# Feed-forward products combined in PSUM, operand order by first use, and gated tiles split early, in a two-layer FP32 trunk on one core

## The chip, the cores and the metric

The kernel runs on one NeuronCore of a Trainium2 chip. The metric is device time in microseconds (us) of one execution. TensorE does the matmuls, VectorE (DVE in the profile) and ScalarE (ACT) the elementwise work, GpSimd (POOL) some additions and the DMAs that add to what is already in SBUF, and SyncE (SP) issues the other loads.

## The reference

Two layers run over 512 tokens of width 1024. The part that the change touches is the gated feed-forward block, which stands twice in a layer, four times in all:

```python
def swiglu_ffn(x, w_in, w_out):
    g, u = jnp.split(x @ w_in, 2, axis=-1)      # w_in: 1024 x 5632
    return (jax.nn.silu(g) * u) @ w_out         # w_out: 2816 x 1024

for i in range(DEPTH):                          # DEPTH = 2
    h = h + 0.5 * swiglu_ffn(rms_norm(h, ffn1_norm[i]), ffn1_w_in[i], ffn1_w_out[i])
    ...   # a state-space mixer and latent attention side by side, added to h
    h = h + 0.5 * swiglu_ffn(rms_norm(h, ffn2_norm[i]), ffn2_w_in[i], ffn2_w_out[i])
    ...   # a gated per-layer input, added to h
```

## The kernel before

Every matrix product is done to FP32 precision out of two parts of each operand: `hi`, a copy in TensorE's reduced FP32 type, and `lo`, what is left of it. A product is hi·hi + hi·lo + lo·hi, three matmuls. Weights come in by DMA as `raw` tiles of 128x1024, and `split_one` makes `hi` on ScalarE (L289) and `lo` on VectorE (L290), two weight tiles ahead of TensorE; there are three buffers of each. Activations are split by `halves` (L420 on ScalarE, L421 on VectorE).

The input projection of a feed-forward block (`ffn`) uses a scheme of seven products in place of eight. The width of 1024 is cut into pairs of 128-row slices, of each slice the 512 tokens into two halves (`HT` = 256). From each pair `NormQ.quarters` makes seven operands of 128x256: four quarters and the sums s1 to s4. There are four pairs, so every product has four operands, one per index k. `quarters` runs while the block before it is still finishing, since its input is that block's result; s1, s2 and s4 are VectorE operations (L540, L541, L543), and s3 a GpSimd operation (L542).

The 5632 columns are done in 11 groups: ten of 512 columns, alternately of the gate (g) and of the up projection (u), and one mixed one (m) at the end. Each group takes the products in the order 1, 2, 7 (of the group before), 5, 4 (of the group before), 3, 6. A product is 24 matmuls of 128x256, with its own weight tile. Some weight tiles are sums of others: GpSimd adds a loaded tile into the old raw tile (L300, 128x1024), or a DMA that GpSimd issues adds to it (L303), always after the `lo` of that raw tile was read.

A product's result collects in a PSUM bank of 128x512 (there are eight). `copied` (L604) brings a result to SBUF on ScalarE. `combined` (L609) adds a bank to such a copy on VectorE, and `finish` applies the norm's factor and the silu (L591, L592) or multiplies with the gate (L595). One of the combinations, called **the old bank's read** from here on, reads the bank `old["a"]` after product 7 of the group before; product 4, which adds to the same bank, has to wait for it. On VectorE it stands as `s<-s,b` (the others are `s<-b,s`), 44 times in the program.

The gated tiles `hid` are then split by `halves` and go through the output projection (`acc_wx`, L407 to L409).

The program text gives an order, but a scheduler orders the instructions of each engine; each engine then runs its own list in order, and waits where an input isn't there.

Of the kernel before, what the change touches and what calls it, by code (L numbers as in the profile page):

```python
# [41 lines left out]
NW = 3  # L42
LOOK_DMA = 3
LOOK_SPLIT = 2
HT = T // 2


# [43 lines left out]
def kernel(ctx: ExitStack, tc: tile.TileContext, a: dict, out: bass.AP):  # L91
# [13 lines left out]
    def S(dt=F32, shape=(P, T)):  # L105
        return slots.get(dt, shape)

    def B(dt=F32):
        return banks.get(dt)
# [291 lines left out]
    def acc_wx(b, w, X, k0=0, first=True, last=True, cs=slice(None)):  # L401
        hi, lo = w
        nk = hi.shape[1]
        for kk in range(nk):
            xh, xl = X[k0 + kk]
            st, en = first and kk == 0, last and kk == nk - 1
            mm(b, lhsT=hi[:, kk, cs], rhs=xh, start=st, stop=False)  # L407
            mm(b, lhsT=hi[:, kk, cs], rhs=xl, start=False, stop=False)  # L408
            mm(b, lhsT=lo[:, kk, cs], rhs=xh, start=False, stop=en)  # L409
# [9 lines left out]
    def halves(src, hi, lo):  # L419
        A.copy(hi, src)  # L420
        V.tensor_tensor(lo, src, hi.bitcast(F32), op=ALU.subtract)  # L421
# [93 lines left out]
    class NormQ(Norm):  # L515
# [20 lines left out]
        def quarters(self, e, o):  # L536
            a11, a21, a12, a22 = e[:, :HT], e[:, HT:], o[:, :HT], o[:, HT:]
            s, t = S(), S()
            s1, s2, s3, s4 = s[:, :HT], s[:, HT:], t[:, :HT], t[:, HT:]
            V.tensor_tensor(s1, a21, a22, op=ALU.subtract)  # L540
            V.tensor_tensor(s2, s1, a11, op=ALU.subtract)  # L541
            G.tensor_tensor(s3, a11, a21, op=ALU.subtract)  # L542
            V.tensor_tensor(s4, a12, s2, op=ALU.add)  # L543
            for p, x in ((1, a11), (2, a12), (5, s1), (6, s2), (4, a22), (7, s3), (3, s4)):
                y = S(F32R)
                halves(x, y[:, :HT], y[:, HT:])
                self.O[p].append(y)
            slots.put(s, t)

        def drop_product(self, p):  # L550
# [8 lines left out]
    def ffn(i, nm, norm, nxt, start=lambda: None, tables=lambda: None, between=lambda: None):  # L559
# [6 lines left out]
        def product(bank, n, p, first):  # L566
            hi, lo = weights((i, nm, n, p))
            ops = norm.O[p]
            for f in range(2):
                o = bank[:, f * HT:(f + 1) * HT]  # L570
                cs = slice(f * P, (f + 1) * P)
                for k in range(4):
                    x = ops[k]
                    more = dict(skip_group_check=not first)
                    mm(o, lhsT=hi[:, k, cs], rhs=x[:, :HT], start=first and f == k == 0, stop=False, **more)  # L575
                    mm(o, lhsT=hi[:, k, cs], rhs=x[:, HT:], start=False, stop=False, **more)  # L576
                    mm(o, lhsT=lo[:, k, cs], rhs=x[:, :HT], start=False, stop=f == 1 and k == 3, **more)  # L577
            if n == NG - 1:
                norm.drop_product(p)

        def two(t):
            return t.rearrange("p (f t) -> p f t", f=2)
# [21 lines left out]
            A.copy(t.ap, b.ap)  # L604
            return t

        def combined(n, a, c, b, t, op, swap=False):
            x, y = (t.ap, b.ap) if swap else (b.ap, t.ap)
            V.tensor_tensor(t.ap, x, y, op=op)  # L609
            finish(n, a, c, t.ap)  # L610
            slots.put(t)

        live = {}
        for n in range(NG + 1):
# [15 lines left out]
                    start()  # L630
            if old:
                product(old["a"], n - 1, 7, False)
                combined(n - 1, 1, 1, old["a"], old["n5"], ALU.subtract, swap=True)
            if n < NG:
                bb = B()
                product(bb, n, 5, True)
# [3 lines left out]
            if old:  # L640
                product(old["a"], n - 1, 4, False)
                finish(n - 1, 1, 0, old["a"].ap)
                banks.put(old["a"])
                live.pop(n - 1)
            if n == NG:
                break
            product(bb, n, 3, False)
# [7 lines left out]
            banks.put(bb)  # L655
            if n == 1:
                tables()
        H = []
        for m in range(KD):
            b = B()  # L660
            for k0 in range(0, KF, 8):
                w = weights((i, nm, "o", m, k0))
                nk = w[0].shape[1]
                if m == 0:
                    for f in range(k0, k0 + nk):
                        hi, lo = S(F32R), S(F32R)
                        for a in range(2):
                            ts = slice(a * HT, (a + 1) * HT)
                            halves(hid[a][f // 2][:, (f % 2) * HT:(f % 2 + 1) * HT], hi[:, ts], lo[:, ts])
                            if f % 2:  # L670
                                slots.put(hid[a][f // 2])
                        H.append((hi, lo))
                acc_wx(b.ap, w, [(p.ap, q.ap) for p, q in H], k0, k0 == 0, k0 + 8 >= KF)
                if m == KD - 1:
                    for p, q in H[k0:k0 + nk]:
                        slots.put(p, q)
            if m == KD - 1:
                between()
            t = tmp()
            V.scalar_tensor_tensor(out=t, in0=b.ap, scalar=0.5, in1=norm.rb.ap, op0=ALU.mult, op1=ALU.mult)  # L680
            banks.put(b)
            V.tensor_tensor(h[m].ap, h[m].ap, t, op=ALU.add)
            nxt.add(h[m].ap)
# [805 lines left out]
```

## Time and profile before

| what | before |
|---|---|
| median of three runs | 2400.01 us (2399.72 to 2402.16) |
| profiled execution | 2397.26 us, of which the span from first to last instruction is 2395.5 us |
| TensorE matmul busy | 2303.1 us, 96% of the span |
| VectorE busy | 1654.9 us, 69% |
| ScalarE busy | 1126.5 us, 47% |
| GpSimd busy | 501.5 us, 21% |
| mean granted TensorE clock | 0.983 |

The profile is that of one execution. TensorE is the engine that is nearly always busy, so the span is its work plus the time in which it waits or runs at a lower clock. 1.76 us of the execution lie outside the span.

### The profile page before, as it was taken

The page shows a single profiled execution, that of the slowest core. Times are in us where ns is not written, and L with a number is a line of the kernel's source. Part 1 is how long each engine was busy: PE and PEld are TensorE (multiplying, and loading weights), DVE is VectorE, ACT ScalarE, POOL GpSimd, SP SyncE. Part 2 cuts the span into 40 slices and gives each one's busy share as a digit, 9 for nine tenths or more (in the row PEclk, how much of TensorE's full clock was granted, in tenths as well). Part 3 has the DMA queues.
Part 4 walks back from the last instruction along what each step waited for, and adds up shares of the span by engine and source line. Part 5 has one row for each costly group of instructions (what it writes and reads, how often), then busy time and mean ns, then how long its engine had stood idle before and what let it go on. Part 6 is the DMA issues. An engine that isn't in the chain of part 4 may idle for free. (4 is left out here: it accounts for less than half of the span.)

```text
span 2395.5 us, 35579 instructions
## 1 busy us (share of the span) xinstructions
PE 2303.1 (96%) x14118; PEld 2056.4 (86%) x14118; DVE 1654.9 (69%) x2440; ACT 1126.5 (47%) x1861; POOL 501.5 (21%) x336
## 2 busy tenths in 40 slices
PE   7999999999999899999999999999999989999998
PEld 6999888878887899978889997888788879998887
DVE  7777744688676777854687875466876777788335
ACT  6544523454455544532554453244544555446224
POOL 3333100123000533300033330011320034332000
PEclk8999999999999899999999999999999989999999
DMA  5665434311222455533356553343112226555322
GB/s 134 134 133 115 104 97 113 88 52 43 69 67 59 105 133 132 111 103 93 91 115 133 124 109 102 90 119 89 33 47 76 70 53 133 132 121 122 97 84 71
DMA packets 339828, 233.32 MB, mean 97 GB/s; under 512 B 20462, under 2 KB 334028, under 8 KB 339660
## 3 DMA queue, kind: packets, MB, share of 16 engines
q1 hardware_dynamic: 288972, 184.89, 26.1%
q0 software_dynamic: 50688, 46.14, 13.1%
q8 instruction: 111, 1.82, 0.3%
q14 instruction: 57, 0.47, 0.1%
HBM read 228.90 MB, written 2.10 MB: 96 GB/s over the span
## 5 line engine op out<-in xcount | busy, mean ns | idle before, releaser
L290 DVE TENSOR_TENSOR lo<-raw,hi 128x1024 fp32r<-128x1024 f32 (+3 forms) x560 | 698.7, 1250 | 431.1 <-ACT hi L289 421.1
L289 ACT CAST hi<-raw 128x1024 fp32r<-128x1024 f32 (+3 forms) x560 | 548.4, 981 | 767.3 <-PE b L408 378.0
L575 PE MATMUL b<-s,hi 128*128 128x256 f32 x2464 | 712.2, 290 | 43.0 <-DVE s L609 27.6
L576 PE MATMUL b<-s,hi 128*128 128x256 f32 x2464 | 708.9, 288 | 7.1 <-DVE s L421 7.1
L577 PE MATMUL b<-s,lo 128*128 128x256 f32 x2464 | 701.6, 288 | 9.1 <-DVE lo L290 9.1
L407 PE MATMUL b<-s,hi 128*128 128x512 f32 (+1 forms) x1498 | 591.8, 397 | 15.9 <-ACT hi L289 15.9
L409 PE MATMUL b<-s,lo 128*128 128x512 f32 (+1 forms) x1498 | 584.3, 391 | 0.0
L408 PE MATMUL b<-s,hi 128*128 128x512 f32 (+1 forms) x1498 | 583.5, 390 | 0.0
L575 PEld LDWEIGHTS b<-s,hi 128*128 128x128 f32 x2464 | 484.5, 197 | 53.1 <-ACT s L420 19.6
L576 PEld LDWEIGHTS b<-s,hi 128*128 128x128 f32 x2464 | 485.0, 197 | 9.6 <-DVE s L421 9.1
L577 PEld LDWEIGHTS b<-s,lo 128*128 128x128 f32 x2464 | 481.1, 197 | 10.7 <-DVE lo L290 10.5
L407 PEld LDWEIGHTS b<-s,hi 128*128 128x128 f32 x1498 | 281.4, 188 | 73.4 <-ACT hi L289 16.8
L409 PEld LDWEIGHTS b<-s,lo 128*128 128x128 f32 x1498 | 280.7, 187 | 59.1 <-DVE lo L290 0.6
L408 PEld LDWEIGHTS b<-s,hi 128*128 128x128 f32 x1498 | 281.4, 188 | 58.0 <-issue 2.9
L300 POOL TENSOR_TENSOR raw<-raw,raw 128x1024 f32<-128x1024 f32 x88 | 224.3, 2549 | 316.3 <-DVE lo L290 315.3
L303 POOL DMA_DIRECT2D raw<-in_ffn_w_in_dram x96 | 125.2, 1346 | 283.4 <-DVE lo L290 214.1
L421 DVE TENSOR_TENSOR s<-s,s 128x256 fp32r<-128x256 f32 (+1 forms) x304 | 143.6, 514 | 12.2 <-ACT s L420 12.0
L492 POOL TENSOR_TENSOR nr<-nv,half 128x4 f32<-128x4 f32 (+1 forms) x14 | 20.9, 1490 | 623.7 <-DVE nv L484 622.9
L420 ACT CAST s<-s 128x256 fp32r<-128x256 f32 (+1 forms) x304 | 110.0, 417 | 56.7 <-PE b L577 29.2
L420 ACT CAST s<-b 128x128 fp32r<-128x128 f32 (+2 forms) x196 | 67.0, 360 | 99.9 <-DVE s L421 38.8
L421 DVE TENSOR_TENSOR s<-b,s 128x128 fp32r<-128x128 f32 (+2 forms) x196 | 75.8, 400 | 30.2 <-ACT s L420 29.1
L592 ACT ACTIVATE s<-s 128x512 f32<-128x512 f32 x80 | 50.1, 631 | 95.7 <-DVE s L591 95.7
(244 smaller groups left out, 2352.2 us busy)
## 6 DMA issues: line engine op xcount, KB each, us to landing
raw<-in_ffn_w_in_dram SPq DMA_DIRECT2D x120, 512.0 KB
raw<-in_ffn_w_in_dram POOLq DMA_DIRECT2D x80, 512.0 KB, 5.9
raw<-in_ffn_w_out_dram SPq DMA_DIRECT2D x64, 512.0 KB
raw<-in_w_in_mix_dram SPq DMA_DIRECT2D x50, 512.0 KB
raw<-in_w_out_mix_dram SPq DMA_DIRECT2D x32, 512.0 KB
raw<-in_ffn_w_out_dram SPq DMA_DIRECT2D x32, 384.0 KB
raw<-in_w_ple_gate_dram SPq DMA_DIRECT2D x16, 512.0 KB
raw<-in_ffn_w_in_dram SPq DMA_DIRECT2D x24, 256.0 KB
```

The source lines that it names most:

```text
L289: A.copy(hi[:, :n], x[:, :n])
L290: V.tensor_tensor(lo[:, :n], x[:, :n], hi[:, :n].bitcast(F32), op=ALU.subtract)
L300: G.tensor_tensor(x[:, :n], x[:, :n], loaded[add][:, :n], op=ALU.add)
L303: lambda dst, src: G.dma_start(out=dst, in_=src, accum_op=ALU.add))
L407: mm(b, lhsT=hi[:, kk, cs], rhs=xh, start=st, stop=False)
L408: mm(b, lhsT=hi[:, kk, cs], rhs=xl, start=False, stop=False)
L409: mm(b, lhsT=lo[:, kk, cs], rhs=xh, start=False, stop=en)
L420: A.copy(hi, src)
L421: V.tensor_tensor(lo, src, hi.bitcast(F32), op=ALU.subtract)
L575: mm(o, lhsT=hi[:, k, cs], rhs=x[:, :HT], start=first and f == k == 0, stop=False, **more)
L576: mm(o, lhsT=hi[:, k, cs], rhs=x[:, HT:], start=False, stop=False, **more)
L577: mm(o, lhsT=lo[:, k, cs], rhs=x[:, :HT], start=False, stop=f == 1 and k == 3, **more)
```

## The change

- `combined` no longer writes its result over the SBUF copy. It writes it in place into the bank (L620 of the new text), and `finish` (L601, L605, and L608 and L610 for the mixed group) reads the bank. The old bank's read writes into a bank of its own, `bd` (L623).
- `quarters` makes the operands one at a time in the order 1, 2, 5, 3, 6, 7, 4, each split as soon as it is made, and s3 is a VectorE operation (L554).
- `product` runs over the operand index k outside and the two column blocks f inside (L584 to L586); before it was the other way round.
- The gated tiles are split by `split_pair`, which `presplit` calls during the last groups where at least `KEEP` = 6 slots stay free; what is left is split ahead of the output projection as before.

Weight splits are L291 in the new text, halves L422, the GpSimd additions L301.

```diff
--- before.py
+++ after.py
@@ -42,6 +42,7 @@
 NW = 3
 LOOK_DMA = 3
 LOOK_SPLIT = 2
+KEEP = 6
 HT = T // 2
 
 
@@ -537,14 +538,22 @@
             a11, a21, a12, a22 = e[:, :HT], e[:, HT:], o[:, :HT], o[:, HT:]
             s, t = S(), S()
             s1, s2, s3, s4 = s[:, :HT], s[:, HT:], t[:, :HT], t[:, HT:]
-            V.tensor_tensor(s1, a21, a22, op=ALU.subtract)
-            V.tensor_tensor(s2, s1, a11, op=ALU.subtract)
-            G.tensor_tensor(s3, a11, a21, op=ALU.subtract)
-            V.tensor_tensor(s4, a12, s2, op=ALU.add)
-            for p, x in ((1, a11), (2, a12), (5, s1), (6, s2), (4, a22), (7, s3), (3, s4)):
+            def ready(p, x):
                 y = S(F32R)
                 halves(x, y[:, :HT], y[:, HT:])
                 self.O[p].append(y)
+
+            ready(1, a11)
+            ready(2, a12)
+            V.tensor_tensor(s1, a21, a22, op=ALU.subtract)
+            ready(5, s1)
+            V.tensor_tensor(s2, s1, a11, op=ALU.subtract)
+            V.tensor_tensor(s4, a12, s2, op=ALU.add)
+            ready(3, s4)
+            ready(6, s2)
+            V.tensor_tensor(s3, a11, a21, op=ALU.subtract)
+            ready(7, s3)
+            ready(4, a22)
             slots.put(s, t)
 
         def drop_product(self, p):
@@ -566,17 +575,18 @@
         def product(bank, n, p, first):
             hi, lo = weights((i, nm, n, p))
             ops = norm.O[p]
-            for f in range(2):
-                o = bank[:, f * HT:(f + 1) * HT]
-                cs = slice(f * P, (f + 1) * P)
-                for k in range(4):
-                    x = ops[k]
+            for k in range(4):
+                x = ops[k]
+                for f in range(2):
+                    o = bank[:, f * HT:(f + 1) * HT]
+                    cs = slice(f * P, (f + 1) * P)
                     more = dict(skip_group_check=not first)
                     mm(o, lhsT=hi[:, k, cs], rhs=x[:, :HT], start=first and f == k == 0, stop=False, **more)
                     mm(o, lhsT=hi[:, k, cs], rhs=x[:, HT:], start=False, stop=False, **more)
                     mm(o, lhsT=lo[:, k, cs], rhs=x[:, :HT], start=False, stop=f == 1 and k == 3, **more)
             if n == NG - 1:
                 norm.drop_product(p)
+                presplit(1)
 
         def two(t):
             return t.rearrange("p (f t) -> p f t", f=2)
@@ -604,11 +614,35 @@
             A.copy(t.ap, b.ap)
             return t
 
-        def combined(n, a, c, b, t, op, swap=False):
-            x, y = (t.ap, b.ap) if swap else (b.ap, t.ap)
-            V.tensor_tensor(t.ap, x, y, op=op)
-            finish(n, a, c, t.ap)
+        def combined(n, a, c, b, t, op, out=None):
+
+            if out is None:
+                V.tensor_tensor(b.ap, b.ap, t.ap, op=op)
+                finish(n, a, c, b.ap)
+            else:
+                V.tensor_tensor(out.ap, t.ap, b.ap, op=op)
+                finish(n, a, c, out.ap)
             slots.put(t)
+
+        H = {}
+        done = [0]
+
+        def split_pair(q):
+            pair = [(S(F32R), S(F32R)) for _ in range(2)]
+            for f in range(2):
+                hi, lo = pair[f]
+                for a in range(2):
+                    ts = slice(a * HT, (a + 1) * HT)
+                    halves(hid[a][q][:, f * HT:(f + 1) * HT], hi[:, ts], lo[:, ts])
+                H[2 * q + f] = pair[f]
+            slots.put(hid[0][q], hid[1][q])
+
+        def presplit(n):
+
+            for _ in range(n):
+                q = len(H) // 2
+                if q < done[0] and len(slots.free) - 4 - (KF - len(hid[0]) * 2) >= KEEP:
+                    split_pair(q)
 
         live = {}
         for n in range(NG + 1):
@@ -630,7 +664,9 @@
                     start()
             if old:
                 product(old["a"], n - 1, 7, False)
-                combined(n - 1, 1, 1, old["a"], old["n5"], ALU.subtract, swap=True)
+                bd = B()
+                combined(n - 1, 1, 1, old["a"], old["n5"], ALU.subtract, out=bd)
+                banks.put(bd)
             if n < NG:
                 bb = B()
                 product(bb, n, 5, True)
@@ -642,6 +678,8 @@
                 finish(n - 1, 1, 0, old["a"].ap)
                 banks.put(old["a"])
                 live.pop(n - 1)
+                done[0] = 2 * KF // 4 if n == NG else n // 2 * 2
+                presplit(1 if n < NG - 1 else 2)
             if n == NG:
                 break
             product(bb, n, 3, False)
@@ -655,25 +693,18 @@
             banks.put(bb)
             if n == 1:
                 tables()
-        H = []
         for m in range(KD):
             b = B()
             for k0 in range(0, KF, 8):
                 w = weights((i, nm, "o", m, k0))
                 nk = w[0].shape[1]
                 if m == 0:
+                    while len(H) < k0 + nk:
+                        split_pair(len(H) // 2)
+                acc_wx(b.ap, w, {f: (p.ap, q.ap) for f, (p, q) in H.items()}, k0, k0 == 0, k0 + 8 >= KF)
+                if m == KD - 1:
                     for f in range(k0, k0 + nk):
-                        hi, lo = S(F32R), S(F32R)
-                        for a in range(2):
-                            ts = slice(a * HT, (a + 1) * HT)
-                            halves(hid[a][f // 2][:, (f % 2) * HT:(f % 2 + 1) * HT], hi[:, ts], lo[:, ts])
-                            if f % 2:
-                                slots.put(hid[a][f // 2])
-                        H.append((hi, lo))
-                acc_wx(b.ap, w, [(p.ap, q.ap) for p, q in H], k0, k0 == 0, k0 + 8 >= KF)
-                if m == KD - 1:
-                    for p, q in H[k0:k0 + nk]:
-                        slots.put(p, q)
+                        slots.put(*H[f])
             if m == KD - 1:
                 between()
             t = tmp()
```

What the scheduler makes of it shows at three places. The first is VectorE in the eighth of the eleven groups of the second feed-forward block, ahead of the old bank's read (the last row in both; `lo` are weight splits, L421 and L422 halves of gated tiles, `b` banks and `s` SBUF tiles). Before:

```order
L290 TENSOR_TENSOR lo220_9573<-raw143_9246,hi220_9572 128x1024
L421 TENSOR_TENSOR s45_593_10291<-s29_536_7771,s36_592_10290 128x256
L421 TENSOR_TENSOR s45_593_10291<-s43_538_7773,s36_592_10290 128x256
L609 TENSOR_TENSOR s15_581_9569<-b4_310_9571,s15_581_9569 128x512
L591 TENSOR_TENSOR s48_577_9536<-s15_581_9569,s5_542_7916 128x512
L290 TENSOR_TENSOR lo221_9605<-raw140_9019,hi221_9604 128x1024
L609 TENSOR_TENSOR s30_575_9438<-s30_575_9438,b5_306_9312 128x512
```

After the change:

```order
L291 TENSOR_TENSOR lo220_9603<-raw143_9275,hi220_9602 128x1024
L620 TENSOR_TENSOR b7_328_9601<-b7_328_9601,s69_585_9599 128x512
L601 TENSOR_TENSOR s34_581_9566<-b7_328_9601,s32_542_7927 128x512
L422 TENSOR_TENSOR s69_596_10058<-s4_537_7783,s65_595_10057 128x256
L422 TENSOR_TENSOR s69_596_10058<-s27_539_7785,s65_595_10057 128x256
L291 TENSOR_TENSOR lo221_9635<-raw140_9047,hi221_9634 128x1024
L623 TENSOR_TENSOR b3_329_9662<-s21_579_9468,b2_323_9341 128x512
```

The halves stand behind the combination and its finish in place of ahead of them. The combination (L620) has a bank as its output, and the finish (L601) one as an input. In the first seven groups the order of these instructions is as before, and only the operands' places are new.

The second is VectorE in the tenth group of the same block, up to the old bank's read (L609 `s<-s,b` before, L623 after). Before:

```order
L421 TENSOR_TENSOR s17_599_10309<-s10_537_7772,s18_598_10308 128x256
L421 TENSOR_TENSOR s17_599_10309<-s56_539_7774,s18_598_10308 128x256
L421 TENSOR_TENSOR s70_605_10327<-s68_548_8181,s32_604_10326 128x256
L421 TENSOR_TENSOR s70_605_10327<-s67_550_8183,s32_604_10326 128x256
L609 TENSOR_TENSOR s33_589_10023<-b4_316_10025,s33_589_10023 128x512
L421 TENSOR_TENSOR s21_607_10333<-s68_548_8181,s23_606_10332 128x256
L421 TENSOR_TENSOR s21_607_10333<-s67_550_8183,s23_606_10332 128x256
L290 TENSOR_TENSOR lo235_10060<-raw146_9471,hi235_10059 128x1024
L609 TENSOR_TENSOR s57_585_9893<-s57_585_9893,b0_312_9766 128x512
```

After the change:

```order
L422 TENSOR_TENSOR s42_610_10226<-s1_561_8658,s40_609_10225 128x256
L422 TENSOR_TENSOR s42_610_10226<-s35_563_8660,s40_609_10225 128x256
L620 TENSOR_TENSOR b2_336_10069<-b2_336_10069,s21_597_10067 128x512
L291 TENSOR_TENSOR lo235_10116<-raw146_9501,hi235_10115 128x1024
L422 TENSOR_TENSOR s23_612_10236<-s5_562_8659,s20_611_10235 128x256
L422 TENSOR_TENSOR s23_612_10236<-s49_564_8661,s20_611_10235 128x256
L422 TENSOR_TENSOR s1_622_10318<-s46_572_9113,s67_621_10317 128x256
L422 TENSOR_TENSOR s1_622_10318<-s30_574_9115,s67_621_10317 128x256
L623 TENSOR_TENSOR b4_337_10143<-s3_589_9925,b1_331_9797 128x512
```

Four halves now stand between the last weight split and the old bank's read, where there were none; two stood ahead of that split, behind the combination. From the combination before this one (some ten rows further up) to the read there are 14 halves in place of 10.

The third is TensorE at the start of the second feed-forward block, where it takes products 1, 2 and 5 (weights 163, 164 and 165) as their operands come. Of product 1, on the first bank, s0_529 before and s26_529 after is the fourth and last operand. Before:

```order
L575 MATMUL b7_283_7775<-s0_529_7747,hi163_7630 128x256
L576 MATMUL b1_284_7807<-s23_519_7679,hi164_7702 128x256
L577 MATMUL b1_284_7807<-s23_519_7679,lo164_7703 128x256
L575 MATMUL b1_284_7807<-s21_530_7750,hi164_7702 128x256
L576 MATMUL b7_283_7775<-s0_529_7747,hi163_7630 128x256
L577 MATMUL b7_283_7775<-s0_529_7747,lo163_7631 128x256
L575 MATMUL b7_283_7775<-s11_496_7533,hi163_7630 128x256
L576 MATMUL b7_283_7775<-s11_496_7533,hi163_7630 128x256
L577 MATMUL b7_283_7775<-s11_496_7533,lo163_7631 128x256
L575 MATMUL b7_283_7775<-s54_507_7604,hi163_7630 128x256
L576 MATMUL b7_283_7775<-s54_507_7604,hi163_7630 128x256
L577 MATMUL b7_283_7775<-s54_507_7604,lo163_7631 128x256
```

After the change:

```order
L584 MATMUL b2_295_7818<-s20_530_7757,hi164_7713 128x256
L585 MATMUL b6_294_7786<-s26_529_7754,hi163_7641 128x256
L586 MATMUL b6_294_7786<-s26_529_7754,lo163_7642 128x256
L584 MATMUL b6_294_7786<-s26_529_7754,hi163_7641 128x256
L585 MATMUL b6_294_7786<-s26_529_7754,hi163_7641 128x256
L586 MATMUL b6_294_7786<-s26_529_7754,lo163_7642 128x256
L585 MATMUL b4_296_7850<-s22_520_7690,hi165_7787 128x256
L586 MATMUL b4_296_7850<-s22_520_7690,lo165_7788 128x256
L584 MATMUL b4_296_7850<-s22_520_7690,hi165_7787 128x256
L585 MATMUL b4_296_7850<-s22_520_7690,hi165_7787 128x256
L586 MATMUL b4_296_7850<-s22_520_7690,lo165_7788 128x256
L584 MATMUL b4_296_7850<-s14_531_7761,hi165_7787 128x256
```

Before, the second column block begins behind the fourth operand with the first operand again (s11_496): 12 of a product's 24 matmuls come behind its last operand's first use. After the change a product's last operand has six matmuls, and they are its last.

## Rows read from the trace of the kernel before

**Rows 1.** What TensorE waited for (longest causes): total us, times, longest us.
```profile
PE b L575 <- DVE s L609: 27.6, 27, 2.5
PE b L407 <- ACT hi L289: 15.9, 4, 4.5
PE b L575 <- ACT s L420: 9.9, 4, 3.6
PE b L577 <- DVE lo L290: 9.1, 6, 2.5
PE b L576 <- DVE s L421: 7.1, 7, 2.1
PE b L575 <- ACT hi L289: 4.1, 2, 2.5
```

**Rows 2.** TensorE at the second FFN's start: window, us, busy (x matmuls), clock, DMA share, GB/s.
```profile
774.00:798.00 24.00, 14.36 (x66) 0.64 0.30 66
```

**Rows 3.** Timeline, VectorE in a plain group: start us, us, line, names, shapes.
```profile
875.54 1.22 DVE L290 TENSOR_TENSOR lo<-raw,hi 128x1024 fp32r<-128x1024 f32 x1 [2.33 <-ACT hi L289]
876.68 0.68 DVE L609 TENSOR_TENSOR s<-b,s 128x512 f32<-128x512 f32 x1
877.40 2.40 DVE L591 TENSOR_TENSOR s<-s,s 128x512 f32<-128x512 f32 x1
879.72 1.21 DVE L290 TENSOR_TENSOR lo<-raw,hi 128x1024 fp32r<-128x1024 f32 x1
880.86 0.68 DVE L609 TENSOR_TENSOR s<-s,b 128x512 f32<-128x512 f32 x1
```

**Rows 4.** Timeline, GpSimd in the same stretch.
```profile
876.85 2.39 POOL L300 TENSOR_TENSOR raw<-raw,raw 128x1024 f32<-128x1024 f32 x1 [6.92 <-DVE lo L290]
```

**Rows 5.** Timeline, TensorE at that read's end; brackets: idle before, releaser.
```profile
880.71 0.28 PE L576 MATMUL b<-s,hi 128*128 128x256 f32 x1
880.83 0.28 PE L577 MATMUL b<-s,lo 128*128 128x256 f32 x1
881.68 0.36 PE L575 MATMUL b<-s,hi 128*128 128x256 f32 x1 [0.57 <-DVE s L609]
```

**Rows 6.** Costs by line and form, VectorE: busy us, mean ns, idle before, releasers.
```profile
L595 DVE TENSOR_TENSOR s<-s,s 128x512 f32<-128x512 f32 x60 | 72.0, 1201 | 2.8 <-ACT s L592 1.2
...
L595 DVE TENSOR_TENSOR s<-b,s 128x512 f32<-128x512 f32 x20 | 13.8, 688 | 6.2 <-PE b L577 6.2
```

**Rows 7.** Timeline, VectorE: a weight split beside the GpSimd addition of 75.16 to 77.55.
```profile
75.59 3.06 DVE L290 TENSOR_TENSOR lo<-raw,hi 128x1024 fp32r<-128x1024 f32 x1
```

**Rows 8.** Timeline, VectorE in the eighth group of the third FFN.
```profile
1381.14 2.96 DVE L421 TENSOR_TENSOR s<-s,s 128x256 fp32r<-128x256 f32 x2
...
1384.74 0.69 DVE L591 TENSOR_TENSOR s<-s,s 128x512 f32<-128x512 f32 x1
```

**Rows 9.** TensorE after that group's read, by window (columns as in Rows 2).
```profile
1387.00:1391.00 4.00, 3.69 (x19) 0.57 0.39 131
```

**Rows 10.** Timeline, TensorE at the read of the tenth group there.
```profile
1430.98 0.36 PE L575 MATMUL b<-s,hi 128*128 128x256 f32 x1 [1.69 <-DVE s L609]
```

**Rows 11.** Timeline, GpSimd at the start of the second FFN.
```profile
776.41 12.92 POOL L542 TENSOR_TENSOR s<-s 128x256 f32<-128x256 f32 x2 [1.61 <-ACT s L528]
```

**Rows 12.** Timeline, ScalarE there.
```profile
789.37 0.41 ACT L420 CAST s<-s 128x256 fp32r<-128x256 f32 x1 [4.43 <-POOL s L542]
```

**Rows 13.** Timeline, TensorE there.
```profile
790.65 0.58 PE L575 MATMUL b<-s,hi 128*128 128x256 f32 x1 [3.65 <-ACT s L420]
791.03 0.41 PE L576 MATMUL b<-s,hi 128*128 128x256 f32 x1
791.24 0.41 PE L577 MATMUL b<-s,lo 128*128 128x256 f32 x1
```

**Rows 14.** Timeline, VectorE there.
```profile
780.90 1.75 DVE L421 TENSOR_TENSOR s<-s,s 128x256 fp32r<-128x256 f32 x5
...
789.80 2.13 DVE L421 TENSOR_TENSOR s<-s,s 128x256 fp32r<-128x256 f32 x1 [1.06 <-ACT s L420]
```

## The prediction

> **What bounds the kernel now.** I read the table of busy times first: TensorE is busy for 96% of the span, so a gain can only come out of its waits, the stretches at the lower clock, or its own work, and the change takes no matmul away. Next, what TensorE waited for [rows 1]. Its waits in the feed-forward blocks fall in three groups. Behind the old bank's read (L609) it stood for 27.6 us in 27 waits, one in most groups. For hi parts of the output projection's weights (L407) it stood for 15.9 us in four waits, one at each block's end. The other four rows (9.9 + 9.1 + 7.1 + 4.1 = 30.2 us) lie nearly all at the four starts, where operands come late: the stretch from 774 to 798 us holds 66 matmuls in 24 us at a clock of 0.64 [rows 2].
>
> Then the timelines of these places. In a plain group VectorE does: weight split, combination, finish, weight split, the old bank's read [rows 3]. GpSimd's addition starts as the first split ends, and takes 2.39 us, from 876.85 to 879.24 [rows 4]. Beside it the combination, which reads a bank, takes 0.68 us as ever. The finish, with both inputs in SBUF, takes 2.40, and ends 0.56 us after the addition. The same finish with an input in PSUM has a mean of 688 ns against 1201 [rows 6]. So a VectorE operation with two SBUF inputs waits for the end of a GpSimd addition that runs. That makes the second split and the read late, and TensorE waits 0.57 us, until 881.68 [rows 5].
>
> **The change, part by part.** The sum is made against the profiled execution's 2397.26 us, 2.75 us under the median of the runs (2400.01).
>
> *Combinations in PSUM, plain groups.* The finish now reads a bank, so it runs beside the addition. But the split behind it has two SBUF inputs and is blocked in its place: where a split met an addition it took 3.06 us [rows 7]. It can go on from 879.24; the read starts 1.14 us after a split does (879.72 to 880.86 [rows 3]), and what a blocked operation has already done gives back some 0.1, so it starts at about 880.3 where it was 880.86. That is 0.5 us per group, not the 1.7 us by which the finish gets shorter. Of the 27.6 us, some 12.8 us lie in 24 waits of the first seven groups of the four blocks (I counted also waits under 0.1 us); taking 0.5 off each, or all of a shorter one, gives 9.5 us, resumption included. It is 8.5 at 0.4 and 10.7 at 0.6.
>
> The price of writing a bank is not in this trace, where VectorE writes SBUF alone. It is bounded from below by nothing (0.68 with a bank or SBUF as input [rows 3, 6]) and from above by a second pass, 0.68 more. For the combination and its finish 0.68 + 0.69 = 1.37 us lie beside 2.39 us of addition, so up to 1.0 us more costs nothing; only the read's own price is on the path. I take nothing, since reading a bank costs nothing. [...]
>
> *Early splits.* They move work on VectorE rather than take any away; the scheduler had already pulled many halves forward. In the eighth group the second half is the blocked one (2.96 us for two [rows 8]), and combination, finish and split come behind it. After, combination and finish run beside the addition, and a half (0.34, by five in 1.75 us [rows 14]) and the split follow it: 0.68 + 0.69 - 0.34 - 0.1 = 0.9 us sooner, in four blocks with waits of 1.54 to 2.51, 3.4 to 3.6 us. In the ninth group, 0.5 us off two waits, 1.0. In the tenth the order goes the other way: 14 halves for 10 ahead of the read, 4 x 0.34 = 1.36 us later at most, 0.7 if part lies in idle time. The read there already ends last (a wait of 1.69 [rows 10]), so 1.0 each, -4.0 in four blocks.
>
> [...]
>
> *Starts.* GpSimd's s3 operations got no turn among VectorE's operations: two took 12.92 us [rows 11]. ScalarE waited 4.43 us for the result [rows 12], and TensorE 3.65 [rows 13], at 790.65. From there it had 45 of the 72 matmuls of products 1, 2 and 5 left, at half clock 0.213 us apart [rows 13], 9.6 us. Now s3 is a VectorE operation (four at a start, 0.34 each like the halves), and only 18 matmuls are left behind the last operands. If these came as they do now, 27 x 0.213 = 5.8 us would go, and with 3.65 of wait 9.4 in all. But VectorE itself is the engine that ends last there: it idled only 1.06 us [rows 14] in 15, the four s3 add 1.4, and GpSimd's addition for product 7 will now meet two-input operations. Between 0 and 9.4 I take 3 for each of the two second blocks, nearer to 0 because of VectorE's row. The waits of each of these two come to 9.6 us, of which rows 13 show the longest; so the first and the third block share some 11 of the 30.2 us. In the first these are mostly waits for weights (both for hi, 4.1, and part of those for lo), with GpSimd's s3 ahead of the additions that make them; for the two together I take 6.5, between 0 and 11. In all 12.5.
>
> *Ends.* The output projection's wait stands behind a weight tile that a GpSimd DMA adds to, and that DMA is issued after the split of the tenth group's tail. Fewer halves are left to do there, but the DMA comes later. I take -1 for 15.9 us, and keep -4 to +5.
>
> Sum: 9.5 + 3.5 + 1.0 - 4.0 + 0 + 12.5 - 1 = 21.5 us, so 2397.3 - 21.5 = 2375.8, say **2376**, with 2366 to 2386 for this case alone.
>
> **The rivals.**
>
> *The starts give nothing* (VectorE is the engine that bounds them, now with 16 more operations). For: its row at 789.80 with 1.06 us idle. Against: 27 fewer matmuls behind the last operand. Then 9 us are left: 2388.
>
> *The starts and waits go almost wholly.* Operands arrive in the order in which TensorE takes them, so it never stands long enough to lose its clock: 9.4 at each second block and 11 at the others, 30, and the plain groups' waits fall to nearly nothing if the split gets in before the addition starts (another 10). For: the operand order now follows the products. Against: the split was blocked in rows 7. 2397 - 30 - 20 = 2347.
>
> *Slower: a write into a bank is dear.* The old bank's read lies on the path in all 44 groups, and its result goes to a bank. If it costs p more, TensorE waits p more in 30 to 44 groups, since waits shorter than p now begin. [...] For: the bank price isn't in the trace. Against: reading a bank costs nothing.
>
> *Nothing changes*: the split's block takes back what the finish gains, and the tenth group and the ends eat the rest. 2394 to 2401.
>
> **How the numbers follow.** Chances: main case 0.50, starts nothing 0.17, nearly all waits gone 0.14, nothing changes 0.08, slower 0.11. The likeliest is 2376. The range takes in the starts' bounds and reaches from 2352 (part of the large case stays out) to 2401; about 0.10 lies below and 0.11 above. A measurement of this kernel tells a difference of about 0.2%, 4.8 us, from none: faster than that holds the first three cases, 0.81, within it 0.08, slower 0.11.
>
> **What would show it.** In the changed profile, right: the finish (L605) near 0.69 us in plain groups, the split (L291) behind it at some 2.3 us where it meets the addition, the old bank's read 1.0 to 1.1 us after the addition's end; TensorE's total behind L623 near 18 us with its longest waits in the tenth groups; combinations L620 and L623 at 0.68 us; the 774 to 798 stretch shorter by 3 us. Wrong: L620 or L623 well above 0.7 us, waits of the plain groups unchanged, VectorE idle at the starts while TensorE waits, or a new wait for a free bank.

## The result: 0.8% faster, with the gain in other places than forecast

| | before | after |
|---|---|---|
| median | 2399.86 us (2399.52 to 2402.16, 4 runs) | 2380.63 us (2379.11 to 2386.05, 4 runs) |
| ratio | | 0.9922, 95% interval 0.9905 to 0.9939 |
| profiled execution, span | 2397.26, 2395.5 us | 2379.11, 2377.4 us |

The forecast was 2376 us, in a range of 2352 to 2401. The span is 18.1 us shorter where 21.5 was the sum.

To see where, I took TensorE's matmul records of the input projections of the four feed-forward blocks (1848 each, all present in both traces) and measured from one start to the start 168 matmuls (one group's worth) later. At full clock and without a wait that is 168 x 0.12 = 20.16 us. The last row ends with the start of the last matmul. The scheduler has put the first 24 to 26 matmuls of the output projection into that stretch too, with the ends' waits (L407 before, L408 after). Worked out from the records, in us:

```
                     block 1          block 2          block 3          block 4       sum of four
matmuls           before  after    before  after    before  after    before  after    before  after
1 to 168           37.09  34.53     37.52  39.22     28.17  26.29     37.31  39.01    140.09 139.05
169 to 336         22.80  25.49     21.21  20.16     20.16  20.27     21.69  20.16     85.86  86.08
337 to 1680       171.95 163.26    166.90 163.67    169.54 162.97    167.45 163.86    675.85 653.76
1681 to 1848       34.09  34.85     33.43  34.21     34.03  34.50     32.18  35.78    133.73 139.34
```

The middle gained 22.1 us (161.28 per block is the floor). The starts gained 1.0 and lost 0.2. The last groups lost 5.6. The other 0.8 us of the span lie outside the table.

What TensorE waited for in the changed kernel (total us, times, longest us), against [rows 1]:

```profile
PE b L584 <- ACT hi L290: 27.0, 15, 6.1
PE b L408 <- ACT hi L290: 19.2, 4, 5.3
PE b L584 <- DVE b L623: 9.6, 14, 2.8
PE b L584 <- ACT s L421: 5.1, 4, 1.8
PE b L586 <- DVE lo L291: 4.8, 2, 4.0
...
PE b L585 <- DVE s L422: 2.0, 2, 1.0
```

Behind the old bank's read (L623) 9.6 us are left of 27.6. But the wait for a hi part of the input weights has grown from 4.1 to 27.0 us: it is the new head of the list. The ends' waits (L408) went from 15.9 to 19.2. By the same records, in the middle stretches the waits over 0.1 us, whatever their cause, fell from 19.0 to 6.0 us, and the time at half clock, by the granted clock, from 10.2 us to none.

A plain group of the changed kernel, VectorE's timeline, and under it GpSimd's of the same stretch, as in [rows 3, 4]:

```profile
827.37 1.23 DVE L291 TENSOR_TENSOR lo<-raw,hi 128x1024 fp32r<-128x1024 f32 x1 [2.24 <-ACT hi L290]
828.51 0.69 DVE L620 TENSOR_TENSOR b<-b,s 128x512 f32<-128x512 f32 x1
829.24 0.69 DVE L601 TENSOR_TENSOR s<-b,s 128x512 f32<-128x512 f32 x1
829.84 2.32 DVE L291 TENSOR_TENSOR lo<-raw,hi 128x1024 fp32r<-128x1024 f32 x1
832.09 0.68 DVE L623 TENSOR_TENSOR b<-s,b 128x512 f32<-128x512 f32 x1
```
```profile
828.68 2.39 POOL L301 TENSOR_TENSOR raw<-raw,raw 128x1024 f32<-128x1024 f32 x1 [8.35 <-DVE lo L291]
```

The addition runs until 831.07. Combination and finish, 0.69 us each, run beside it. The split behind them is blocked instead (2.32 us), and the read starts 1.02 us after the addition's end, where it was 1.62. That is the step as forecast.

The costs by line and form, VectorE (busy us, mean ns), first two rows of the kernel before, then the changed kernel:

```profile
L609 DVE TENSOR_TENSOR s<-b,s 128x512 f32<-128x512 f32 x88 | 60.1, 682 | 3.5 <-PE b L577 3.1 <-ACT s L420 0.4
...
L609 DVE TENSOR_TENSOR s<-s,b 128x512 f32<-128x512 f32 x44 | 29.7, 675 | 0.4 <-PE b L577 0.4
```
```profile
L291 DVE TENSOR_TENSOR lo<-raw,hi 128x1024 fp32r<-128x1024 f32 x474 | 669.2, 1415 | 381.9 <-ACT hi L290 380.6
...
L620 DVE TENSOR_TENSOR b<-b,s 128x512 f32<-128x512 f32 x88 | 60.9, 692 | 0.0
L605 DVE TENSOR_TENSOR s<-b,s 128x512 f32<-128x512 f32 x80 | 55.1, 689 | 8.6 <-PE b L586 6.2 <-ACT s L602 0.7
...
L623 DVE TENSOR_TENSOR b<-s,b 128x512 f32<-128x512 f32 x44 | 30.1, 684 | 6.8 <-PE b L586 6.8
```

The combinations that write into a bank take 692 and 684 ns, some 10 ns more than the same operations into SBUF in the kernel before (682 and 675).

The start of the second block, in this order GpSimd, ScalarE and TensorE, and the longest stretch of VectorE there, against [rows 11 to 14]:

```profile
778.32 10.15 POOL L301 TENSOR_TENSOR raw<-raw,raw 128x1024 f32<-128x1024 f32 x1 [11.12 <-DVE lo L291]
```
```profile
788.50 1.04 ACT L290 CAST hi<-raw 128x1024 fp32r<-128x1024 f32 x1 [4.93 <-POOL raw L301]
```
```profile
789.60 0.58 PE L584 MATMUL b<-s,hi 128*128 128x256 f32 x1 [6.13 <-ACT hi L290]
```
```profile
780.09 3.10 DVE L422 TENSOR_TENSOR s<-s,s 128x256 fp32r<-128x256 f32 x9
...
785.05 1.22 DVE L291 TENSOR_TENSOR lo<-raw,hi 128x1024 fp32r<-128x1024 f32 x1
786.18 0.69 DVE L620 TENSOR_TENSOR b<-b,s 128x512 f32<-128x512 f32 x1
```

GpSimd has no s3 any more, and so its weight addition for product 6 is at the head of its list at 778.32. It ends at 788.47, 2.2 us after the end of VectorE's last operation with two SBUF inputs (785.05 + 1.22 = 786.27). In the plain group above an addition takes 2.39 in all, so this one made next to no headway during the eight us before. ScalarE waits 4.93 us for its result, and TensorE 6.13 us for the hi part that ScalarE makes of it.

### The profile page after: what moved, and what is told of

Same layout as the page of the kernel before. It is cut to its first block, busy times and chain, and to the rows that moved or that the text cites. A ratio compares the mean times of both kernels' runs of the same rounds, so it can differ in the third digit from the quotient of the medians.

```text
span 2377.4 us, 35557 instructions
## 1 busy us (share of the span) xinstructions
PE 2294.2 (97%) x14118; PEld 2052.0 (86%) x14118; DVE 1636.6 (69%) x2456; ACT 1126.3 (47%) x1860; POOL 479.5 (20%) x320
## 5 line engine op out<-in xcount | busy, mean ns | idle before, releaser
L291 DVE TENSOR_TENSOR lo<-raw,hi 128x1024 fp32r<-128x1024 f32 (+3 forms) x560 | 727.6, 1302 | 419.2 <-ACT hi L290 417.8
L584 PE MATMUL b<-s,hi 128*128 128x256 f32 x2464 | 709.6, 289 | 41.9 <-ACT hi L290 27.0
L586 PE MATMUL b<-s,lo 128*128 128x256 f32 x2464 | 699.4, 287 | 4.9 <-DVE lo L291 4.8
L408 PE MATMUL b<-s,hi 128*128 128x512 f32 (+1 forms) x1498 | 592.6, 398 | 19.2 <-ACT hi L290 19.2
L584 PEld LDWEIGHTS b<-s,hi 128*128 128x128 f32 x2464 | 483.2, 196 | 49.9 <-ACT hi L290 34.2
L586 PEld LDWEIGHTS b<-s,lo 128*128 128x128 f32 x2464 | 479.4, 196 | 5.5 <-DVE lo L291 5.5
L408 PEld LDWEIGHTS b<-s,hi 128*128 128x128 f32 x1498 | 281.6, 188 | 77.0 <-ACT hi L290 20.0
L301 POOL TENSOR_TENSOR raw<-raw,raw 128x1024 f32<-128x1024 f32 x88 | 246.0, 2796 | 333.6 <-DVE lo L291 317.3
L422 DVE TENSOR_TENSOR s<-s,s 128x256 fp32r<-128x256 f32 (+1 forms) x304 | 139.4, 501 | 3.8 <-ACT s L421 3.6
L421 ACT CAST s<-s 128x256 fp32r<-128x256 f32 (+1 forms) x304 | 111.6, 416 | 55.8 <-DVE s L422 15.1
L421 ACT CAST s<-b 128x128 fp32r<-128x128 f32 (+2 forms) x196 | 67.2, 361 | 99.7 <-DVE s L422 38.7
L422 DVE TENSOR_TENSOR s<-b,s 128x128 fp32r<-128x128 f32 (+2 forms) x196 | 76.0, 402 | 30.1 <-ACT s L421 28.9
L416 PE MATMUL b<-hi,s 128*128 128x512 f32 (+1 forms) x208 | 78.0, 375 | 0.0
```

Source lines behind the costliest of these rows:

```text
L291: V.tensor_tensor(lo[:, :n], x[:, :n], hi[:, :n].bitcast(F32), op=ALU.subtract)
L301: G.tensor_tensor(x[:, :n], x[:, :n], loaded[add][:, :n], op=ALU.add)
```

## Experiments

Each is timed against the kernel before on its own chip, where before had medians of 2405.88 to 2406.17 us; ratios are what can be compared. On one of these chips the changed kernel ran again, and there, too, it is at 0.9918 (0.9905 to 0.9931).

> The changed kernel once more, unaltered, on the chip of the next three runs, so that they can be set against it. Both theories: 0.988 to 0.995 of the kernel before on this chip.

**PSUM combinations alone.** The kernel before with the new `combined` and the bank for the old bank's read, nothing else:

```diff
...
-            V.tensor_tensor(t.ap, x, y, op=op)
-            finish(n, a, c, t.ap)
...
+            if out is None:
+                V.tensor_tensor(b.ap, b.ap, t.ap, op=op)
+                finish(n, a, c, b.ap)
+            else:
+                V.tensor_tensor(out.ap, t.ap, b.ap, op=op)
+                finish(n, a, c, out.ap)
...
+                bd = B()
+                combined(n - 1, 1, 1, old["a"], old["n5"], ALU.subtract, out=bd)
+                banks.put(bd)
```

> The kernel before with the PSUM combinations alone (in-place combination, finish out of the bank, a bank of its own for the old bank's read). Theory (the gain in the middle of the blocks comes from the finish running beside the GpSimd addition): the waits behind the old bank's read fall from 27.6 us to 10 to 14, the plain groups' reads start 1.0 to 1.1 us after the addition's end, and the time is 10 to 16 us under before, 2384 to 2390. Starts and ends as before. Rival (the gain needs the early splits too, since they free VectorE ahead of the read): under 5 us.

Measured: 0.9923 (0.9910 to 0.9937), median 2386.32. That is the whole change's ratio, and 19.9 us, more than the 10 to 16 expected. In the times, PSUM alone accounts for the gain. The waits behind the read were still 20.9 us in the profiled run, over the 10 to 14 expected (the read is L613 here):

```profile
PE b L575 <- DVE b L613: 20.9, 18, 2.4
```

This run (2393.27) was the slowest of six, but that need not be the reason: the changed kernel with the columns first (below) has 22.4, where the changed kernel itself has 9.6 and 12.0 in its two profiles. So the fall from 27.6 to 9.6 is not the PSUM combinations' alone; it hangs on the order of the products' loops too.

**Starts alone.** The kernel before with the new `quarters` and `product`:

```diff
...
-            G.tensor_tensor(s3, a11, a21, op=ALU.subtract)
...
+            V.tensor_tensor(s3, a11, a21, op=ALU.subtract)
...
-            for f in range(2):
-                for k in range(4):
+            for k in range(4):
+                for f in range(2):
```

> The kernel before with the operand order, s3 on VectorE and the products over the operands first, and nothing else. Theory (what s3 on GpSimd cost comes back as a starved GpSimd addition for the weights of product 6): within 3 us of before, 2397 to 2402, with a wait of 5 to 7 us for a hi part at the starts of the second blocks. Rival (the starts do gain and something else in the full change loses it again): 8 to 13 us faster, and no wait for hi over 3 us at the starts.

Measured: 0.9998 (0.9988 to 1.0008). TensorE's waits in it:

```profile
PE b L583 <- DVE s L617: 33.5, 32, 2.6
PE b L583 <- ACT hi L289: 23.2, 10, 6.1
```

The 6.1 us wait for a hi part is there without any PSUM edit: it belongs to the new starts. The theory held, and the forecast's 12.5 us for the starts did not come.

**No early splits.** The changed kernel with them switched off:

```diff
-KEEP = 6
+KEEP = 99
```

> The changed kernel without early splits (all gated tiles are split ahead of the output projection in the program text, as before). Theory (the scheduler pulls the halves forward by itself, and the early splits only move them ahead of a weight split): the waits of the eighth groups grow by 0.5 to 1 us each, the tenth groups' change by under 1 us each, 2380 to 2386, that is 0 to 6 us slower than the full change. Rival (the early splits carry the ends): the ends' waits of 19.2 us grow by 5 us or more, 2387 or more.

Measured: 0.9909 (0.9896 to 0.9922). The time was to be 0 to 6 us longer; it is not longer, so early splits bring nothing here that can be told from no change. The ends' waits stay (18.0 us in four). The waits behind the read are 17.6 us where the full change has 9.6, without a longer time, so the sum of one kind of wait says little about the time by itself.

**First group's additions on VectorE.** In the changed kernel:

```diff
-                G.tensor_tensor(x[:, :n], x[:, :n], loaded[add][:, :n], op=ALU.add)
+                (V if units[j][0][2] == 0 else G).tensor_tensor(x[:, :n], x[:, :n], loaded[add][:, :n], op=ALU.add)
```

> The changed kernel with the weight additions of each block's first group on VectorE in place of GpSimd; nothing else is changed. Theory (GpSimd's addition starves behind VectorE's two-input operations at the starts): the 6.1 us waits for a hi part at the two second blocks' starts go, VectorE has 1.2 us more to do for each, and the time is 6 to 14 us under the full change, 2367 to 2375. Rival (VectorE is the bound there whatever GpSimd does): operands come as late as the weights did, and the time is within 3 us of the full change, 2378 to 2384.

> The changed kernel with the weight additions of each block's first group on VectorE, once more, on the chip of the next three. Both theories: 0.983 to 0.990 of the kernel before.

Measured: 0.9866 (0.9853 to 0.9878), and again 0.9869 (0.9852 to 0.9885), median 2373.78 and 2373.47. Against the changed kernel's 0.9918 to 0.9922 that is 0.5%, some 12 us, as expected: the price of having the first groups' eight additions, the two starved ones among them, on GpSimd. The first 72 matmuls of the second and fourth blocks took 19.8 us where they had taken 23.1. What TensorE waits for next there is a half that VectorE makes:

```profile
787.18 0.58 PE L585 MATMUL b<-s,hi 128*128 128x256 f32 x1 [2.84 <-DVE s L422]
```

**Before, without GpSimd's additions.** Products 4 and 6 then use incomplete weights, so this is a time for the cause alone:

```diff
-                G.tensor_tensor(x[:, :n], x[:, :n], loaded[add][:, :n], op=ALU.add)
```

> The kernel before with the GpSimd additions of weight tiles left out, so that products 4 and 6 are done with weights that miss a part. Theory (the finish waits for the running addition): the finish with two SBUF inputs falls from 1.0 to 1.2 us to 0.69 us on the mean, the waits behind the old bank's read fall from 27.6 us to under 10, and the time is 15 to 30 us under before. Rival (the finish is long for its SBUF operands by themselves): it stays over 0.95 us on the mean, and the gain is under 8 us.

Measured: 0.9772 (0.9755 to 0.9788), a gain of 53 us, more than expected. The finish with SBUF inputs alone:

```profile
L594 DVE TENSOR_TENSOR s<-s,s 128x512 f32<-128x512 f32 x60 | 41.5, 692 | 2.4 <-ACT s L591 0.5
L590 DVE TENSOR_TENSOR s<-s,s 128x512 f32<-128x512 f32 x60 | 41.2, 692 | 1.6
```

692 ns in place of 1201 [rows 6]: the operands never were the cost, the running addition was. Measured as in the table, all 32 stretches of 168 matmuls between 337 and 1680 (eight in each block) take 20.16 us, and of the waits behind the old bank's read 0.3 us are left:

```profile
PE b L574 <- DVE s L608: 0.3, 1, 0.3
```

So GpSimd's additions were the cause of nearly all of these waits, not of a part.

**Products with the columns first.** The changed kernel with the two loops of `product` as before:

```diff
-            for k in range(4):
-                for f in range(2):
+            for f in range(2):
+                for k in range(4):
```

> The changed kernel with the products' loops as before (column blocks outside, operands inside). Theory (a weight part is what comes last at the second blocks' starts, so it matters little how many matmuls are left behind the last operand): 0 to 4 us slower than the changed kernel, most of it at the third block's start. Rival (the operand order of the matmuls is worth the 5.8 us per second block that was predicted): 8 us slower or more.

Measured: 0.9936 (0.9920 to 0.9953), median 2390.76, 3.1 us over the changed kernel on the same chip (2387.66). The intervals overlap, so it is a hint that fits the theory: at the third block's start the first 72 matmuls took 17.59 us against 14.92, and at the second block's the 6.1 us wait was 3.0: TensorE came to it after 72 matmuls in place of 67. The waits behind the read changed more than the time did:

```profile
PE b L584 <- DVE b L623: 22.4, 14, 2.6
```

Against that, the waits for a hi part were 17.1 us (25.5 in the changed kernel on the same chip) and the ends' 12.3 (19.8).

**s3 on GpSimd again.** In the changed kernel:

```diff
-            V.tensor_tensor(s3, a11, a21, op=ALU.subtract)
+            G.tensor_tensor(s3, a11, a21, op=ALU.subtract)
```

> The changed kernel with s3 on GpSimd again. Theory (GpSimd starves behind VectorE's two-input operations, whatever it has to do): s3 takes 5 us or more at the second blocks' starts, the weight addition behind it in GpSimd's queue comes later still, and the time is 2 to 10 us over the changed kernel. Rival (s3 and the addition fit side by side since VectorE has four operations less): within 2 us of the changed kernel or faster.

Measured: 0.9924 (0.9912 to 0.9936), median 2388.43, 0.8 us over the changed kernel, not told from it. That is the rival's number, but the theory's mechanism. GpSimd's timeline at the second block's start:

```profile
771.29 12.91 POOL L554 TENSOR_TENSOR s<-s 128x256 f32<-128x256 f32 x2 [1.61 <-ACT s L529]
784.17 2.36 POOL L301 TENSOR_TENSOR raw<-raw,raw 128x1024 f32<-128x1024 f32 x1
```

s3 starves as before (12.91 us for two here, 12.92 in [rows 11]), and the addition behind it takes 2.36 us, where in the changed kernel, with no s3 ahead of it, it took 10.15. One of the two is long in either kernel, and no difference in price can be told.

**All additions on VectorE**, in the changed kernel and in the kernel before, by the same line:

```diff
-                G.tensor_tensor(x[:, :n], x[:, :n], loaded[add][:, :n], op=ALU.add)
+                V.tensor_tensor(x[:, :n], x[:, :n], loaded[add][:, :n], op=ALU.add)
```

> The changed kernel with all weight additions on VectorE, so that GpSimd only issues DMAs in the blocks. Theory (what an addition takes on VectorE, about 1.2 us, is no more than what the running GpSimd addition costs the split that it blocks, 2.33 in place of 1.22 us): VectorE's busy time changes by less than 40 us though it gets 106 us of additions, the mean split falls from 1415 to about 1235 ns, the waits behind the old bank's read stay under 12 us, and the time is 0.980 to 0.988 of before. Rival (the addition stands ahead of the old bank's read on VectorE and makes it late in every group): those waits grow to 20 us or more, and the time is over 0.990 of before.

> The kernel before with all weight additions on VectorE and nothing else. Theory (the PSUM combinations help only because they pass a running GpSimd addition): the finish takes 0.69 us again, the waits behind the old bank's read fall to between 8 and 20 us, and the time is 0.985 to 0.994 of before, so that most of the change's gain can be had without PSUM combinations. Rival (VectorE has no room for 106 us of additions): 0.997 or more.

Measured: 0.9807 (0.9793 to 0.9822) on the changed kernel, 0.9809 (0.9794 to 0.9824) on the kernel before, which needs no other edit. The first is as expected, the second better than the 0.985 to 0.994 expected. Both beat both kernels. In the changed kernel with all additions on VectorE, busy times and two rows of VectorE:

```profile
PE 2290.9 (97%) x14118; PEld 2049.9 (87%) x14118; DVE 1611.2 (68%) x2544; ACT 1130.5 (48%) x1860; POOL 243.6 (10%) x232
```
```profile
L291 DVE TENSOR_TENSOR lo<-raw,hi 128x1024 fp32r<-128x1024 f32 x474 | 582.6, 1231 | 401.3 <-ACT hi L290 398.1 <-PE b L586 2.2
L301 DVE TENSOR_TENSOR raw<-raw,raw 128x1024 f32<-128x1024 f32 x88 | 107.5, 1222 | 2.1
```

VectorE took on 107.5 us of additions, and its busy time fell, from the changed kernel's 1636.6 to 1611.2 us. Its splits alone got 86.6 us shorter (669.2 to 582.6). So beside the 88 GpSimd additions it had been busy, or blocked, for 107.5 + 25.4 = 132.9 us more than without them, 1.5 us for each, where doing one takes 1.22. In the kernel before with this line, the finish is back at 0.69 us, with both inputs in SBUF, and of the waits behind the old bank's read 1.3 us are left:

```profile
L595 DVE TENSOR_TENSOR s<-s,s 128x512 f32<-128x512 f32 x60 | 41.0, 685 | 1.5 <-ACT s L592 0.9
```

Since the two are equal in time, with the additions gone from GpSimd the PSUM combinations and the rest of the change show no gain. GpSimd also issues DMAs, which then no longer stand behind an addition in its list; how much of the gain that gives is not separated here.

**The last group's weights by a plain load.** On top of all additions on VectorE in the changed kernel:

```diff
                 add = {6: 3, 4: 2}.get(p)
+                if n == len(GROUPS) - 1 and p == 7:
+                    at[n, 0] = (None, raw(4, 256, *quarter(n, 0, 1)))
+                    add = 0
```

> The changed kernel with all additions on VectorE, and the last group's weights for product 7 made out of a plain load and a VectorE addition in place of a DMA of GpSimd that adds in SBUF. Theory (the ends wait for that DMA): the waits of the output projection for a hi part fall from 16 to 20 us to under 8, and the time is 0.972 to 0.983 of before. Rival (the ends wait for the last gated tile or a slot in any case): under 3 us beside the kernel with all additions on VectorE.

Measured: 0.9802 (0.9787 to 0.9816), 2.7 us by the medians beside all additions on VectorE, not told from it. The ends' waits were 8.0 us here and 6.5 there, so the rival's number held, and the DMA is not what the ends wait for here: with the additions moved their waits had already fallen from 19.2. In the kernel before with the additions moved they are still 16.9, so it takes more than the additions to shorten them; which part of the change does was not tried.

## Why the prediction was right, and where it was not

*PSUM price: right.* I took nothing for a bank write; it is 10 ns (692 and 684 against 682 and 675, above). For a bank as source I took nothing either: a finish has 689 ns with one (L605 of the changed kernel), and without 692 (L594 of the kernel before without GpSimd's additions) or 0.69 us where no addition runs [rows 8].

*Plain and eighth groups: right in mechanism, small in size.* The read's shift of 0.5 to 0.6 us came as worked out. The sum of plain, eighth and ninth groups was 9.5 + 3.5 + 1.0 = 14.0 us; the middle gained 22.1. In the eighth group of the third block the wait of 2.5 us fell to 1.04, by more than the 0.9 that I had taken, and the half-clock patch behind it, where the clock was 0.57 on the mean of 4 us [rows 9], went (the granted clock is 1.00 from 1369 to 1374):

```profile
1370.32 0.36 PE L584 MATMUL b<-s,hi 128*128 128x256 f32 x1 [1.04 <-DVE b L623]
```

The + 0 in the sum stands for the clock, and no run shows that term. By the granted clock of the two profiles, the input projections' time at half clock went from 51.2 to 47.8 us in the first 336 matmuls, from 10.2 to none in the middle, and from 20.5 to 23.9 in the last 168. Matmuls stood 0.21 us apart at half clock [rows 13] and 0.12 at full [rows 5], so the middle's 10.2 us are worth some 4.4 us, an estimate from these two distances, and a part of the 8.1 that I had too few there.

*Tenth group: wrong.* "14 halves for 10 ahead of the read, 4 x 0.34 = 1.36 us later at most." VectorE's timeline there, second block, before and after the change:

```profile
1000.51 1.23 DVE L290 TENSOR_TENSOR lo<-raw,hi 128x1024 fp32r<-128x1024 f32 x1 [0.35 <-ACT hi L289]
1001.65 3.63 DVE L421 TENSOR_TENSOR s<-s,s 128x256 fp32r<-128x256 f32 x4
1005.21 0.68 DVE L609 TENSOR_TENSOR s<-b,s 128x512 f32<-128x512 f32 x1
1005.81 0.74 DVE L421 TENSOR_TENSOR s<-s,s 128x256 fp32r<-128x256 f32 x2
1006.48 1.21 DVE L290 TENSOR_TENSOR lo<-raw,hi 128x1024 fp32r<-128x1024 f32 x1
1007.62 0.67 DVE L609 TENSOR_TENSOR s<-s,b 128x512 f32<-128x512 f32 x1
```
```profile
991.26 1.22 DVE L291 TENSOR_TENSOR lo<-raw,hi 128x1024 fp32r<-128x1024 f32 x1
992.39 0.76 DVE L422 TENSOR_TENSOR s<-s,s 128x256 fp32r<-128x256 f32 x2
993.06 0.70 DVE L620 TENSOR_TENSOR b<-b,s 128x512 f32<-128x512 f32 x1
993.66 2.83 DVE L291 TENSOR_TENSOR lo<-raw,hi 128x1024 fp32r<-128x1024 f32 x1
996.42 1.42 DVE L422 TENSOR_TENSOR s<-s,s 128x256 fp32r<-128x256 f32 x4
997.76 0.68 DVE L623 TENSOR_TENSOR b<-s,b 128x512 f32<-128x512 f32 x1
```

GpSimd's addition (after the change 2.86 us from 992.56) starts with the first split's end, and what counts is what stands behind that: six halves, a combination and a split in both kernels. The four additional halves stand ahead of it. From that split's end to the read it is 5.3 us after the change and 5.9 before. The wait behind the read became 0.2 us, with 1.07 us for a hi part ahead of it, where it had been 1.5 to 2.0. This hangs on the order that the scheduler makes: with the columns first (the run above) seven halves stand behind that split in the second block, and TensorE waits 2.3 to 2.6 us behind the reads of the four tenth groups, as long as I had forecast.

*Starts: wrong, the step that failed.* "Between 0 and 9.4 I take 3 for each of the two second blocks", and 6.5 for the first and third together, 12.5 us in all. The first 336 matmuls gained 0.8 in the four blocks: the two second blocks (2 and 4 in the table) lost 0.6 and 0.2, the first and third together gained 1.6. The rival in which the starts give nothing was right about the starts for the wrong reason: not VectorE's load but GpSimd's addition bounds them. I had named the mechanism (the addition "will now meet two-input operations", though for product 7, whose weights come by an adding DMA; it is product 6's) and given it no price. It was 10.15 us long in the second block, and without the first groups' additions on GpSimd the kernel was 12 us shorter. In those runs the two second blocks' first 336 matmuls are 2.4 to 3.6 us shorter than in the kernel before's profile, about the 3 forecast. Only a part of that can be the new order's: in the kernel before with all additions on VectorE, and the old order, they are 2.3 and 0.7 us shorter.

*Last groups: near in sum.* For the tenth groups and the ends the forecast had -4.0 - 1.0 = -5.0 us; the last row of the table lost 5.6. The ends' waits grew by 3.3 us (15.9 to 19.2), and the tenth groups' fell by 1.6 (6.8 to 5.2). The rest goes with 3.4 us more at half clock there (20.5 to 23.9 us), and with four matmuls more of the output projection that now stand in the stretch. Why the ends' waits grew stays open; with the columns first they were 12.3.

So the total was near by luck: the starts' 11.7 us too many and the last groups' 0.6 us of further loss stood against 8.1 us too few in the middle and the 0.8 us outside the table.

## What to carry to other kernels

An operation that takes two or three times its usual length with the same operands is a sign to look at what another engine does at that moment, and to work out what it would cost to move that other work, in place of rearranging around it: here one line that moves GpSimd's additions to VectorE is worth 1.9%, and the rearrangement 0.8%. When a starved operation is moved away, price what takes its place at the head of that engine's list. And where a blocked stretch is tied to an event, count instructions from that event, not from a convenient landmark.

## What the hardware showed that I had not expected

At the start of the second block GpSimd's addition made next to no headway beside a run of VectorE operations: it took 10.15 us, where the one in the plain group took 2.39. From 778.32 to 786.27 all of VectorE's operations there have two SBUF inputs and follow each other without a gap (busy for 7.80 of 7.80 us from 778.40), and the addition ended 2.2 us after the last of these. In the run with s3 on GpSimd again it was two s3 operations that took 12.91 us there. VectorE was held up in its turn: a split took 2.32 us beside a running addition, and 1.23 where none ran. Moving all 88 additions to VectorE made it less busy, not more (1636.6 to 1611.2 us).
